# Input projection of a hybrid layer on one core: the weights of q, k, the convolution and the gates in column sets of 256 instead of 512

## The chip, the cores and the metric

The kernel runs on one NeuronCore of a Trainium2 chip. The metric is the device time of one execution in microseconds (us); it is compared by the median of several runs. PE is the matrix engine, PEld its weight loads, DVE the vector engine, ACT the scalar engine, POOL the GpSimd engine, SP the queue that issues nearly all DMAs.

## The reference, cut to what matters

One layer over 2048 tokens of width 1024. A normed input `u` goes through one wide projection; its columns are cut into q, k, v, a gate g, a low-rank gate, and the three parts of a gated short convolution. The rest (output projection, feed-forward, embedding gate) is not touched by the change.

```python
u = _rmsnorm(h, ln1_g[i])
proj = u @ w_in[i]
q, k, v, g, g_lr, cb, cc, cx = jnp.split(proj, offsets, axis=-1)
gate_logits = (g_lr @ w_gate_up[i] + b_gate[i]).astype(jnp.float32)
log_a = jax.nn.log_sigmoid(gate_logits) / GATE_NORMALIZER
...
o = _gla_chunked(qh, kh, vh, ah).astype(x.dtype)      # chunked linear attention (GLA)
o = _rmsnorm(o, gn_g[i]) * jax.nn.silu(gh)
y = cb * _causal_depthwise_conv(cc * cx, conv_w[i])
mix = jnp.concatenate([o, y], axis=-1) @ w_out[i]
```

## The kernel before, in words

All matrix products run in a split form: each float32 operand is cut into a high and a low part, and three products (high*high, high*low, low*high) are summed in PSUM. To cut a weight tile, ACT casts the raw float32 tile to the high part (L105) and DVE subtracts it from the raw one for the low part (L106). The pair of parts stands in a tile of the pool `hl`, the raw weights in a tile of the pool `raw`.

The first of three phases (`mixing_phase`) takes the tokens in four blocks of 512, numbered 0 to 3 here. In each block `mixing` does, in this order: the values v with the low-rank gate (weights as the moving operand), then 20 *units* of the transposed projection: four for q and k, eight for the convolution (`cc` and `cx` in turn), four for g and four for cb. A unit is 24 matmuls of 128x512 (8 chunks of the 1024 input features, k-chunks, by 3 passes) into one PSUM bank, followed by a small evacuation. Then `block` does the output projection with `w_out`, which also loads the next block's input, norms it and turns it.

`tick` is called in the middle and at the end of each unit. It advances the generator `gla`, which puts the attention's own small matmuls between the units: the gate logits (L370, in the middle of the second q/k unit), the score products of six levels (L417 for the first two, L427 for the others) and of pairs (L454), and then the state passes. Ahead of them stands a chain on ACT, POOL and DVE: absolute value, Exp and Ln of the logits (L371 to L375), differences on POOL (L377), a scan on DVE (L378), and per level two differences on POOL (L399, L400), an Exp on ACT (L401) and two products on DVE (L402, L403).

Weights come in *sets* by `weights`: a set of 512 columns is loaded by `load_pair`, two k-chunks to a raw tile (512 KB, rows of 2 KB; for the convolution two DMAs of 256 KB with rows of 1 KB), and `split` cuts one k-chunk of 512 columns at a time, so that a set is eight `hl` tiles, each of which serves all four units of the set.

```python
pools(st, {"hl": 11, "raw": 4, "w4": 13})
```

The pool `hl` has 11 tiles and `raw` has 4; a new tile takes the place of the one 11 (4) before it and waits until that one's last reader is done. In this phase only PE's instructions stand in the order in which the program is written. The order on ACT, DVE, POOL and SP is made by a scheduler ahead of the run, by a cost model of its own; on the chip each engine then runs its list strictly in order.

Of the kernel before, what the change touches and what calls it, by code (L numbers as in the profile page):

```python
# [8 lines left out]
F32 = mybir.dt.float32  # L9
F32R = mybir.dt.float32r  # L10
# [4 lines left out]
P = 128  # L15
S = 2048
D = 1024
NK = D // P
# [6 lines left out]
O_Q, O_V, O_G, O_LR, O_CB, O_CC, O_CX = 0, 512, 1024, 1536, 1552, 2064, 2576  # L25
# [14 lines left out]
def hybrid_layer(ctx: ExitStack, tc: tile.TileContext,  # L40
                 x, p, ln1_g, w_in, w_gate_up, b_gate, conv_w, gn_g, w_out, ln2_g,
                 w_up, w_down, ln3_g, w_pg, w_pp, lnf_g, out):
    nc = tc.nc
    x, out = x[0], out[0]
    p = p[0, 0]
    w_in, w_gate_up, b_gate, conv_w = w_in[0], w_gate_up[0], b_gate[0], conv_w[0]
# [5 lines left out]
    pl = {}  # L52
# [40 lines left out]
    def load_pair(src, k0, width, segs):  # L93

        raw = pl["raw"].tile([P, 2, width], F32, name="raw")
        o = 0
        for c, n in segs:
            nc.sync.dma_start(out=raw[:, :, o:o + n],
                              in_=src[k0 * P:(k0 + 2) * P, c:c + n].rearrange("(k p) n -> p k n", p=P))
            o += n  # L100
        return raw

    def split(raw, width):
        hl = pl["hl"].tile([P, 2, width], F32R, name="hl")
        nc.scalar.copy(out=hl[:, 0, :], in_=raw)  # L105
        nc.vector.tensor_tensor(out=hl[:, 1, :], in0=raw, in1=hl[:, 0, :].bitcast(F32), op=ALU.subtract)  # L106
        return hl

    def weights(src, segs, k0=0, nk=NK, between=None):
        width = sum(n for _, n in segs)  # L110
        tiles = []
        for k in range(k0, k0 + nk, 2):
            raw = load_pair(src, k, width, segs)
            if between:
                between(k)
            for i in range(2):
                tiles.append(split(raw[:, i, :], width))
        return lambda k, s: tiles[k][:, s, :]

# [31 lines left out]
    def unit(out_ap, lhs, rhs, nk, done=None, ticks=True):  # L153

        product(out_ap, lhs, rhs, nk, mid=True)
        if done is not None:
            done()
        if ticks:
            tick()

    def split_into(hi, lo, src):
        nc.scalar.copy(out=hi, in_=src)  # L162
        nc.vector.tensor_tensor(out=lo, in0=src, in1=hi.bitcast(F32), op=ALU.subtract)  # L163
# [4 lines left out]
    def uT_at(u, sl):  # L168
        return lambda k, s: u[k // 4][:, k % 4, s, sl]

    def tok_of(ti):
        return slice(ti * P, (ti + 1) * P)

    full = slice(0, T)
# [121 lines left out]
    def mixing_phase(st):  # L296
# [251 lines left out]
        def mixing(b, u1, first):  # L548

            vt = [w4([P, 2, 512]) for _ in range(2)]  # L550
            wv = weights(w_in, [(O_V, 512), (O_LR, 16)], between=first)

            def v_done(ps, ti, n):
                dst = vt[ti // 2][:, ti % 2, :]
                if n == 0:
                    nc.scalar.copy(out=dst[:, 0:264], in_=ps[:, 0:264])
                    return
                lr = tiny.tile([P, 16], F32, name="lr")
                nc.vector.tensor_copy(out=lr, in_=ps[:, 248:264])
                nc.scalar.copy(out=dst[:, 264:512], in_=ps[:, 0:248])  # L560

                def low_rank():
                    tp = tr_bank()
                    nc.tensor.transpose(out=tp[0:16, 0:P], in_=lr, identity=ident)
                    nc.vector.tensor_copy(out=lrT[0:16, ti * P:(ti + 1) * P], in_=tp[0:16, 0:P])
                later(2, low_rank)

            for ti in range(NT):
                if first is not None:
                    first(8 + ti)  # L570
                cols = [slice(n * 264, (n + 1) * 264) for n in range(2)]
                banks = [mm_bank() for _ in range(2)]
                lhs = uT_at(u1, tok_of(ti))
                if first is not None and ti == 0:
                    for k in range(NK):
                        for n in range(2):
                            for i, (a, c) in enumerate(PASSES):
                                nc.tensor.matmul(out=banks[n][:, 0:264], lhsT=lhs(k, a), rhs=wv(k, c)[:, cols[n]],
                                                 start=(k == 0 and i == 0), stop=(k == NK - 1 and i == 2))
                    v_done(banks[0], ti, 0)  # L580
                    v_done(banks[1], ti, 1)
                    continue
                for n in range(2):
                    unit(banks[n][:, 0:264], lhs, lambda k, s: wv(k, s)[:, cols[n]], NK,
                         lambda: v_done(banks[n], ti, n))
            mix = [None, None]
            wq = weights(w_in, [(O_Q, 512)])
            qT = w4([P, 2, T])
            kT = w4([P, 2, T])
            gsT = [w4([P, 2, T]) for _ in range(2)]  # L590
            side[0] = gla(qT, kT, vt, gsT, mix)
            for j in range(4):
                ps = mm_bank()

                def qk_done():
                    if j < 2:
                        nc.scalar.mul(out=qT[:, j, :], in_=ps, mul=0.125)
                    else:
                        nc.scalar.copy(out=kT[:, j - 2, :], in_=ps)
                unit(ps, lambda k, s: wq(k, s)[:, j * P:(j + 1) * P], uT_at(u1, full), NK, qk_done)  # L600

            mix[1] = big([P, 4, 2, T], F32R)
            yt = [w4([P, 2, T]) for _ in range(2)]
            for g in range(2):
                wc = weights(w_in, [(O_CC + g * 256, 256), (O_CX + g * 256, 256)])
                for jj in range(2):
                    j = g * 2 + jj
                    z = t2([P, T + 2])
                    pc = mm_bank()

                    def cc_done():
                        nc.gpsimd.tensor_copy(out=z[:, 0:2], in_=halo[:, j, :])
                        nc.scalar.copy(out=z[:, 2:T + 2], in_=pc)
                    unit(pc, lambda k, s: wc(k, s)[:, jj * P:(jj + 1) * P], uT_at(u1, full), NK, cc_done)
                    px = mm_bank()

                    def cx_done():
                        nc.vector.tensor_tensor(out=z[:, 2:T + 2], in0=px, in1=z[:, 2:T + 2], op=ALU.mult)
                        nc.gpsimd.tensor_copy(out=halo[:, j, :], in_=z[:, T:T + 2])
                        y = yt[g][:, jj, :]  # L620
                        nc.vector.tensor_scalar(out=y, in0=z[:, 2:T + 2], scalar1=cw[:, 2, j:j + 1], scalar2=None,
                                                op0=ALU.mult)
                        nc.vector.scalar_tensor_tensor(out=y, in0=z[:, 1:T + 1], scalar=cw[:, 1, j:j + 1], in1=y,
                                                       op0=ALU.mult, op1=ALU.add)
                        nc.vector.scalar_tensor_tensor(out=y, in0=z[:, 0:T], scalar=cw[:, 0, j:j + 1], in1=y,
                                                       op0=ALU.mult, op1=ALU.add)
                    unit(px, lambda k, s: wc(k, s)[:, 256 + jj * P:256 + (jj + 1) * P], uT_at(u1, full), NK, cx_done)
            wg = weights(w_in, [(O_G, 512)])
            for h in range(4):
                ps = mm_bank()  # L630

                def g_done():
                    gs = t2([P, T])
                    nc.scalar.activation(out=gs, in_=ps, func=AF.Silu)
                    nc.vector.tensor_scalar(out=gsT[h // 2][:, h % 2, :], in0=gs, scalar1=gng, scalar2=None, op0=ALU.mult)
                unit(ps, lambda k, s: wg(k, s)[:, h * P:(h + 1) * P], uT_at(u1, full), NK, g_done)

            wb = weights(w_in, [(O_CB, 512)])
            for j in range(4):
                ps = mm_bank()  # L640

                def cb_done():
                    y = yt[j // 2][:, j % 2, :]
                    last["cb"] = nc.vector.tensor_tensor(out=y, in0=ps, in1=y, op=ALU.mult)
                    split_into(mix[1][:, j, 0, :], mix[1][:, j, 1, :], y)
                unit(ps, lambda k, s: wb(k, s)[:, j * P:(j + 1) * P], uT_at(u1, full), NK, cb_done)
            while side[0] is not None:
                tick()
            return mix
# [30 lines left out]
        u1 = new_uT()  # L680
# [48 lines left out]
        for b in range(NB):  # L729
            u1 = block(b, u1, start if b == 0 else None)  # L730
# [691 lines left out]
```

## Time and profile before

| what | value |
|---|---|
| median of 3 runs | 2488.64 us (2488.27 to 2496.26) |
| the profiled execution: time, span | 2492.06 us, 2490.3 us |
| PE busy, share of the span | 2380.4 us, 96% |
| mean granted TensorE clock | 0.983 |
| DVE, ACT, POOL busy | 56%, 39%, 28% |
| raw weight loads from `w_in` of 512 KB / 256 KB | 64 / 64 |

The profile is one execution on the chip. In its groups a row has line, engine, operation, out<-in with the shapes, the count, the busy time, the mean time of one, and the idle time of the engine ahead of it with what ended it. The first phase ends at about 957 us.

### The profile page before, as it was taken

What the parts mean: (1) busy time and instruction counts of PE and PEld (TensorE: products, weight loads), DVE (VectorE), ACT (ScalarE), POOL (GpSimd) and SP (SyncE); (2) the same over time, 40 slices, a digit from 0 to 9 for tenths busy, and PEclk for the clock granted to TensorE, in tenths of its full rate; (3) what the DMA queues carried; (4) which work ended last, traced back from release to release, by engine and by line L of the source; (5) the groups of instructions that cost most, each with busy time, mean ns of one, the idle gap of its engine ahead of it and who ended that gap; (6) DMA issues with size and microseconds to landing.
All of it is one profiled execution on the core that took longest, in us unless ns stands there. A gap on an engine that the chain in (4) does not pass through costs nothing.

```text
span 2490.3 us, 31389 instructions
## 1 busy us (share of the span) xinstructions
PE 2380.4 (96%) x11752; PEld 1946.6 (78%) x11752; DVE 1394.1 (56%) x1676; ACT 974.7 (39%) x1533; POOL 698.6 (28%) x604
## 2 busy tenths in 40 slices
PE   7999999899999996999999999999999999999976
PEld 6777878777887784788888888888887888788765
DVE  4656465556646641655555664445546555655758
ACT  4434433443344333522222332222224344435555
POOL 3301210431103014244343243244522105301421
PEclk9999999999999997999999999999999999999988
DMA  4226323731542248854354576557757669756997
GB/s 154 68 68 217 103 72 135 217 99 59 170 153 68 68 145 274 277 175 164 135 181 162 196 260 217 202 200 256 259 203 288 201 220 296 276 189 239 330 298 273
DMA packets 274761, 471.08 MB, mean 189 GB/s; under 512 B 22688, under 2 KB 146096, under 8 KB 274608
## 3 DMA queue, kind: packets, MB, share of 16 engines
q1 hardware_dynamic: 272112, 460.66, 54.8%
q0 software_dynamic: 2496, 8.41, 1.4%
q8 instruction: 92, 1.51, 0.2%
q14 instruction: 61, 0.50, 0.1%
HBM read 326.92 MB, written 142.08 MB: 188 GB/s over the span
## 4 chain that ended last, share of the span: by engine, by line
PE 64%; DMA 7%; issue 3%; DVE 3%; ACT 2%; POOL 2%; SPq 0%; POOLq 0%; ACTq 0%; DVEq 0%
PE mm L148 46%; PE ps L1069 15%; DMA ur<-up 1%; DMA mr<-hid 1%; DMA mr<-u 1%; PE g L427 1%; DMA out_dram<-w 1%; POOL as L218 1%; DMA h<-h_out 1%; DMA w<-up 1%; POOL w L218 0%; DMA emb<-w 0%; DVE hl L106 0%; ACT mh L162 0%; PE ps L1102 0%
## 5 line engine op out<-in xcount | busy, mean ns | idle before, releaser
L1069 PE MATMUL ps<-wh,mh 128*128 128x512 f32 x2496 | 578.1, 392 | 23.2 <-ACT mh L162 16.0
L1069 PEld LDWEIGHTS ps<-wh,mh 128*128 128x128 f32 x2496 | 468.7, 189 | 126.3 <-ACT mh L162 18.0
L148 PE MATMUL mm<-uT,hl 128*128 128x512 f32 x1920 | 481.7, 405 | 10.1 <-DVE hl L106 6.3
L148 PE MATMUL mm<-uT,wu 128*128 128x512 f32 x2112 | 482.3, 389 | 0.0
L148 PEld LDWEIGHTS mm<-uT,wu 128*128 128x128 f32 x2112 | 396.5, 188 | 82.2
L148 PEld LDWEIGHTS mm<-uT,hl 128*128 128x128 f32 x1920 | 356.5, 190 | 105.1 <-DVE hl L106 11.8
L148 PE MATMUL mm<-U,wu 128*128 128x512 f32 x1584 | 364.5, 390 | 3.1 <-DVE v L218 3.1
L148 PEld LDWEIGHTS mm<-U,wu 128*128 128x128 f32 x1584 | 298.5, 188 | 65.6 <-issue 3.5
L163 DVE TENSOR_TENSOR wu<-raw,wu 128x1024 fp32r<-128x1024 f32 x154 | 218.1, 1416 | 209.3 <-ACT wu L162 208.8
L148 PE MATMUL mm<-hl,uT 128*128 128x512 f32 (+1 forms) x1584 | 301.0, 349 | 3.4 <-DVE uT L163 2.1
L148 PEld LDWEIGHTS mm<-hl,uT 128*128 128x128 f32 x1584 | 252.1, 190 | 42.8 <-DVE uT L163 2.7
L162 ACT CAST wu<-raw 128x1024 fp32r<-128x1024 f32 x154 | 161.5, 1050 | 304.7 <-PE mm L148 222.1
L163 DVE TENSOR_TENSOR wh<-wr,wh 128x1024 fp32r<-128x1024 f32 x111 | 141.3, 1273 | 235.8 <-ACT wh L162 235.0
L218 DVE TENSOR_TENSOR v<-mm,v 128x512 f32<-128x512 f32 x220 | 150.9, 687 | 151.4 <-PE mm L148 150.6
L218 POOL TENSOR_TENSOR v<-v,v 128x512 f32<-128x512 f32 x88 | 137.5, 1563 | 302.4 <-DMA hid<-v 262.0
L162 ACT CAST wh<-wr 128x1024 fp32r<-128x1024 f32 x111 | 110.8, 998 | 248.3 <-PE ps L1069 185.5
L106 DVE TENSOR_TENSOR hl<-raw,hl 128x512 fp32r<-128x512 f32 (+1 forms) x260 | 183.6, 744 | 26.5 <-ACT hl L105 26.3
L105 ACT CAST hl<-raw 128x512 fp32r<-128x512 f32 (+1 forms) x260 | 153.8, 622 | 61.3 <-PE mm L148 30.3
L218 POOL TENSOR_TENSOR raw<-raw 128x1024 f32<-128x1024 f32 x44 | 107.4, 2451 | 224.7 <-issue 149.3
L163 DVE TENSOR_TENSOR mh<-mr,mh 128x1024 fp32r<-128x1024 f32 x111 | 144.2, 1299 | 5.7 <-ACT mh L162 5.2
L162 ACT CAST mh<-mr 128x1024 fp32r<-128x1024 f32 x111 | 110.6, 996 | 9.4 <-DMA mr<-hid 7.2
L218 POOL TENSOR_TENSOR ur<-ur 128x512 f32<-128x512 f32 x60 | 93.5, 1559 | 31.7 <-DMA ur<-in_w_ple_gate_dram 26.9
(190 smaller groups left out, 1882.6 us busy)
## 6 DMA issues: line engine op xcount, KB each, us to landing
raw<-in_w_gate_upffn_dram SPq DMA_DIRECT2D x77, 512.0 KB, 4.8
hid<-v SPq DMA_DIRECT2D x154, 256.0 KB, 3.4
mr<-hid SPq DMA_DIRECT2D x70, 512.0 KB, 4.8
raw<-in_w_in_dram SPq DMA_DIRECT2D x64, 512.0 KB, 4.4
wu<-raw SPq DMA_DIRECT2D x44, 512.0 KB, 3.0
raw<-wu SPq DMA_DIRECT2D x44, 512.0 KB, 5.8
wr<-wd SPq DMA_DIRECT2D x40, 512.0 KB, 3.7
w<-in_x_dram SPq DMA_DIRECT2D x32, 512.0 KB, 9.0
```

The source lines that it names most:

```text
L105: nc.scalar.copy(out=hl[:, 0, :], in_=raw)
L106: nc.vector.tensor_tensor(out=hl[:, 1, :], in0=raw, in1=hl[:, 0, :].bitcast(F32), op=ALU.subtract)
L148: nc.tensor.matmul(out=out_ap, lhsT=lhs(k, a), rhs=rhs(k, b), start=(start and k == 0 and i == 0), stop=(k == nk - 1 and i == 2), **kw)
L162: nc.scalar.copy(out=hi, in_=src)
L163: nc.vector.tensor_tensor(out=lo, in0=src, in1=hi.bitcast(F32), op=ALU.subtract)
L218: return e.tensor_tensor(out=out, in0=a, in1=b, op=op)
L427: nc.tensor.matmul(out=sp[par][:, a, :], lhsT=X[r, c], rhs=X[r, c], start=True, stop=True)
L1069: nc.tensor.matmul(out=bk[n][t], lhsT=M[a][:, j, tok_of(t)], rhs=W[c][:, j, :], start=(on is None and k == 0 and i == 0), stop=(k == nk - ...
```

## The change

A new helper `columns` takes the place of `weights` for all of the input projection but the values. A set is 256 columns: two raw tiles, each with four k-chunks, and four `hl` tiles, each with two k-chunks. A set serves two units and is asked for just ahead of them. For the convolution the set of one j holds 128 columns of `cc` and 128 of `cx`. The number of raw tiles, of casts and subtractions, their sizes (128x512) and the bytes are as before. The output projection and the values keep `weights`.

```diff
+    def columns(src, segs, nk=NK):
+
+        tiles = []
+        for k in range(0, nk, 4):
+            raw = pl["raw"].tile([P, 4, 256], F32, name="raw")
+            o = 0
+            for c, n in segs:
+                nc.sync.dma_start(out=raw[:, :, o:o + n],
+                                  in_=src[k * P:(k + 4) * P, c:c + n].rearrange("(k p) n -> p k n", p=P))
+                o += n
+            for i in range(0, 4, 2):
+                hl = pl["hl"].tile([P, 2, 2, 256], F32R, name="hl")
+                split_into(hl[:, 0], hl[:, 1], raw[:, i:i + 2, :])
+                tiles.append(hl)
+        return lambda k, s: tiles[k // 2][:, s, k % 2, :]
...
-            wq = weights(w_in, [(O_Q, 512)])
...
             for j in range(4):
                 ps = mm_bank()
+                if j % 2 == 0:
+                    wq = columns(w_in, [(O_Q + j * P, 256)])
...
-                unit(ps, lambda k, s: wq(k, s)[:, j * P:(j + 1) * P], uT_at(u1, full), NK, qk_done)
+                unit(ps, lambda k, s: wq(k, s)[:, tok_of(j % 2)], uT_at(u1, full), NK, qk_done)
...
             for g in range(2):
-                wc = weights(w_in, [(O_CC + g * 256, 256), (O_CX + g * 256, 256)])
                 for jj in range(2):
                     j = g * 2 + jj
+                    wc = columns(w_in, [(O_CC + j * P, P), (O_CX + j * P, P)])
...
-                    unit(pc, lambda k, s: wc(k, s)[:, jj * P:(jj + 1) * P], uT_at(u1, full), NK, cc_done)
+                    unit(pc, lambda k, s: wc(k, s)[:, 0:P], uT_at(u1, full), NK, cc_done)
...
-                    unit(px, lambda k, s: wc(k, s)[:, 256 + jj * P:256 + (jj + 1) * P], uT_at(u1, full), NK, cx_done)
+                    unit(px, lambda k, s: wc(k, s)[:, P:2 * P], uT_at(u1, full), NK, cx_done)
...
-            wg = weights(w_in, [(O_G, 512)])
...
+                if h % 2 == 0:
+                    wg = columns(w_in, [(O_G + h * P, 256)])
...
-            wb = weights(w_in, [(O_CB, 512)])
...
+                if j % 2 == 0:
+                    wb = columns(w_in, [(O_CB + j * P, 256)])
```

The lists of the engines show what the scheduler made of it. PE's list is the same, instruction for instruction. Three places differ that matter below. In these lists the numbers tell one tile from another; a raw or `hl` tile is given when it is loaded or cut.

The first is ACT at the passage from q/k to the convolution, here in block 1. Before, the casts of the convolution's first set (raw_2739, raw_2748, raw_2757; the two of its first raw tile stand further up) from its fourth tile on stand behind two of the Exps of the levels (L401):

```order
L371 ACTIVATE uT_2619<-g_2650,bg_233 128x512
L374 ACT_TABLE_LOAD
L374 ACTIVATE uT_2619<-uT_2619 128x1024
L597 ACTIVATE w4_2598<-mm_2633 128x512
L375 ACT_TABLE_LOAD
L375 ACTIVATE uT_2619<-uT_2619 128x1024
L387 ACT_TABLE_LOAD
L387 ACTIVATE ebl_2673<-w4_2618 128x8
L401 ACTIVATE uT_2619<-uT_2619 128x1024
L599 COPY w4_2599<-mm_2675 128x512
L401 ACTIVATE uT_2619<-uT_2619 128x1024
L105 CAST hl_2745<-raw_2739 128x512
```

With the change the lines of the file are 16 higher (L387 is the old L371, L391 the old L375, L403 the old L387) and the list at the same place is:

```order
L614 ACTIVATE w4_2566<-mm_2570 128x512
L178 CAST hl_2745<-raw_2739 128x512
L178 CAST hl_2809<-raw_2806 128x512
L387 ACTIVATE uT_2603<-g_2630,bg_233 128x512
L387 ACTIVATE uT_2603<-g_2634,bg_233 128x512
L390 ACT_TABLE_LOAD
L390 ACTIVATE uT_2603<-uT_2603 128x1024
L614 ACTIVATE w4_2566<-mm_2617 128x512
L391 ACT_TABLE_LOAD
L391 ACTIVATE uT_2603<-uT_2603 128x1024
L178 CAST hl_2812<-raw_2806 128x512
L178 CAST hl_2818<-raw_2815 128x512
```

Here hl_2745 is the fourth and last tile of the convolution's first set (j = 0), and hl_2809, hl_2812 and hl_2818 are three of the four of its second (j = 1): they have moved ahead of the Exps of the levels, and two of them ahead of the logits' first operation.

The second is SP at the end of a block, here block 1: after the loads of `w_out` come those of the residual rows and gains, then the first weights of the next block's values (raw_4222).

```order
L98 DMA raw_3952<-in_w_out_dram 128x2x512
L188 DMA w4_3724<-in_ln2_g_dram 128x1024
L256 DMA w4_3726<-in_x_dram 128x1024
L256 DMA w4_3728<-in_x_dram 128x1024
L256 DMA w4_3730<-in_x_dram 128x1024
L256 DMA w4_3732<-in_x_dram 128x1024
L188 DMA w4_3734<-in_ln1_g_dram 128x1024
L256 DMA w4_3796<-in_x_dram 128x1024
L98 DMA raw_4222<-in_w_in_dram 128x2x512
```

With the change:

```order
L98 DMA raw_3952<-in_w_out_dram 128x2x512
L98 DMA raw_4222<-in_w_in_dram 128x2x512
L204 DMA w4_3724<-in_ln2_g_dram 128x1024
L272 DMA w4_3726<-in_x_dram 128x1024
L272 DMA w4_3728<-in_x_dram 128x1024
L272 DMA w4_3730<-in_x_dram 128x1024
L272 DMA w4_3732<-in_x_dram 128x1024
L204 DMA w4_3734<-in_ln1_g_dram 128x1024
L272 DMA w4_3796<-in_x_dram 128x1024
```

The load of 512 KB for the values has moved ahead of the seven loads of rows and gains.

The third is DVE in the convolution, block 1, between two score products of one level (the copies by mask32 empty the two PSUM banks of the attention, and the next score products wait for both). Before:

```order
L429 COPY_PREDICATED s_sb01_241<-mask32_244,g_3058 128x512
L618 TENSOR_TENSOR t2_2959<-mm_3036,t2_2959 128x512
L621 TENSOR_SCALAR w4_2729<-t2_2959,cw_234 128x512
L623 SCALAR_TENSOR_TENSOR w4_2729<-t2_2959,cw_234,w4_2729 128x512
L429 COPY_PREDICATED s_sb10_242<-mask32_244,g_3086 128x512
L625 SCALAR_TENSOR_TENSOR w4_2729<-t2_2959,cw_234,w4_2729 128x512
L429 COPY_PREDICATED s_sb11_243<-mask32_244,g_3087 128x512
```

With the change:

```order
L445 COPY_PREDICATED s_sb01_241<-mask32_244,g_3040 128x512
L179 TENSOR_TENSOR hl_3345<-raw_3340,hl_3345 128x512
L635 TENSOR_TENSOR t2_2941<-mm_3018,t2_2941 128x512
L179 TENSOR_TENSOR hl_3350<-raw_3348,hl_3350 128x512
L638 TENSOR_SCALAR w4_2729<-t2_2941,cw_234 128x512
L445 COPY_PREDICATED s_sb10_242<-mask32_244,g_3068 128x512
L640 SCALAR_TENSOR_TENSOR w4_2729<-t2_2941,cw_234,w4_2729 128x512
L445 COPY_PREDICATED s_sb11_243<-mask32_244,g_3069 128x512
```

Two subtractions of weight tiles (hl_3345, hl_3350) now stand among them, and one step of the convolution (L642, the old L625) has moved behind the last copy.

More of the change, by code (lines that the diff above doesn't have):

```diff
@@ L635, in g_done @@
                     nc.vector.tensor_scalar(out=gsT[h // 2][:, h % 2, :], in0=gs, scalar1=gng, scalar2=None, op0=ALU.mult)
-                unit(ps, lambda k, s: wg(k, s)[:, h * P:(h + 1) * P], uT_at(u1, full), NK, g_done)
-            wb = weights(w_in, [(O_CB, 512)])
+                unit(ps, lambda k, s: wg(k, s)[:, tok_of(h % 2)], uT_at(u1, full), NK, g_done)
             for j in range(4):
                 ps = mm_bank()
+                if j % 2 == 0:
+                    wb = columns(w_in, [(O_CB + j * P, 256)])
                 def cb_done():
@@ L645, in cb_done @@
                     split_into(mix[1][:, j, 0, :], mix[1][:, j, 1, :], y)
-                unit(ps, lambda k, s: wb(k, s)[:, j * P:(j + 1) * P], uT_at(u1, full), NK, cb_done)
+                unit(ps, lambda k, s: wb(k, s)[:, tok_of(j % 2)], uT_at(u1, full), NK, cb_done)
             while side[0] is not None:
```

## The prediction

> **What bounds the kernel now.** I read the page's first part, its groups, the idle time ahead of PE's groups, then PE's timeline of the first phase and a table of stretches.
>
> ```profile
> PE 2380.4 (96%) x11752; PEld 1946.6 (78%) x11752; DVE 1394.1 (56%) x1676; ACT 974.7 (39%) x1533; POOL 698.6 (28%) x604
> L148 PE MATMUL mm<-uT,hl 128*128 128x512 f32 x1920 | 481.7, 405 | 10.1 <-DVE hl L106 6.3
> ```
>
> PE is busy for 96% of the span, and no other engine is near it, so time can only be won where PE stands still or runs slowly. The second row is the group that the change feeds: all 80 units, 1920 matmuls. PE idled 10.1 us ahead of them, mostly until DVE had finished a weight tile. The timeline of block 2 shows where:
>
> ```profile
> 516.72 16.66 PE L148 MATMUL mm<-uT,hl 128*128 128x512 f32 x69
> 533.89 0.72 PE L148 MATMUL mm<-uT,hl 128*128 128x512 f32 x2 [0.51 <-ACT hl L105]
> 535.80 0.97 PE L148 MATMUL mm<-uT,hl 128*128 128x512 f32 x3 [1.19 <-DVE hl L106]
> 537.25 0.96 PE L148 MATMUL mm<-uT,hl 128*128 128x512 f32 x3 [0.48 <-DVE hl L106]
> 538.81 18.64 PE L148 MATMUL mm<-uT,hl 128*128 128x512 f32 x67 [0.60 <-DVE hl L106]
> 557.39 0.68 PE L417 MATMUL g<-uT 64*64 64x64 f32 x16
> ```
>
> The stretch starts behind the gate logits, in the middle of the second q/k unit. 12 matmuls end that unit, 48 more are the last two of q/k, so the 69th is the ninth of the first convolution unit: PE has used three k-chunks, and waits for the fourth tile of the convolution's set. ACT's timeline says why it is late:
>
> ```profile
> 516.46 0.69 ACT L371 ACTIVATE uT<-g,bg 128x512 f32<-128x512 f32 x1 [3.05 <-PE g L370]
> 530.23 1.06 ACT L401 ACTIVATE uT<-uT 128x1024 f32<-128x1024 f32 x1 [1.93 <-POOL uT L400]
> 531.20 0.57 ACT L599 COPY w<-mm 128x512 f32<-128x512 f32 x1
> 532.27 1.06 ACT L401 ACTIVATE uT<-uT 128x1024 f32<-128x1024 f32 x1 [0.51 <-POOL uT L400]
> 533.24 2.68 ACT L105 CAST hl<-raw 128x512 fp32r<-128x512 f32 x5
> ```
>
> The five casts run at 533.24, behind two Exps that wait for POOL. They could not have been put much earlier: with 11 tiles, the fourth tile of this set takes the place of the first of q/k, which is read until the last q/k unit. The stretch from the logits to the first score product, 144 matmuls, compares the blocks (rows 1 to 4), with a run of 96 undisturbed matmuls (row 5) and three short windows inside the stretches of blocks 1, 2 and 3 (length, PE busy, ..., granted clock):
>
> ```profile
> core 0: us, PE busy (x) PEld busy (x) DVE busy (x) ACT busy (x) POOL busy (x), PEclk, DMA share, GB/s
> 55.43:93.26 37.83, 35.10 (x146) 26.78 (x145) 23.34 (x27) 19.87 (x28) 17.34 (x14) 1.00 0.19 56
> 281.90:320.70 38.80, 36.63 (x146) 27.66 (x145) 25.06 (x27) 21.08 (x29) 18.22 (x14) 0.96 0.19 54
> 516.72:557.39 40.67, 37.89 (x147) 28.76 (x145) 25.06 (x27) 21.09 (x29) 18.24 (x14) 0.92 0.18 52
> 745.77:784.74 38.97, 36.52 (x147) 27.50 (x145) 25.06 (x27) 21.09 (x29) 18.23 (x14) 0.96 0.18 54
> 656.30:678.70 22.40, 22.40 (x97) 17.99 (x96) 8.22 (x12) 7.14 (x14) 2.04 (x4) 1.00 0.81 284
> 302.50:306.00 3.50, 3.49 (x8) 2.30 (x9) 3.50 (x5) 2.63 (x5) 0.87 (x1) 0.51 0.65 197
> 538.10:544.90 6.80, 6.20 (x15) 4.79 (x15) 6.80 (x12) 2.45 (x4) 0.11 (x1) 0.50 0.67 191
> 766.80:770.20 3.40, 3.11 (x8) 1.89 (x8) 3.40 (x6) 2.20 (x4) 0.45 (x1) 0.50 0.64 197
> ```
>
> The stall costs more than its idle time: right behind it, in three of four blocks, the clock granted to PE is halved for 3.4 or 6.8 us.
>
> **The change part by part.** *The fourth tile.* An undisturbed matmul takes 22.40 / 96 = 0.2333 us, 144 of them 33.60. The four stretches lose 37.83 - 33.60 = 4.23, 5.20, 7.07 and 5.37 us, 21.87 in all. A part is not the stall's: the first 69 matmuls take 16.66 us where (68 x 0.2333) + 0.39 for the last one's own duration would be 16.26; this 0.40 at the start stays, 1.6 in four blocks. That leaves 20.3 us to win: idle time (37.83 - 35.10) + 2.17 + 2.78 + 2.45 = 10.1; half speed over 3.5, 6.8 and 3.4 us, about 1.7 + 3.4 + 1.7 = 6.8; the remaining 3.4 is the refilling of PE's pipeline after each stop.
>
> Will it be won? In the change the convolution's first set has four tiles. The first three take the places of value tiles. The fourth takes that of q/k's first tile, which now is read for the last time early in the second unit, not in the fourth; its cast (hl_2745) stands ahead of the logits' first operation, where ACT idled 3.05 us (516.46), some 17 us ahead of PE's need at 533.4. Of the second set, needed two units (11.2 us) later still, three casts stand ahead of the Exps too, the last behind two of them. Had that one come as late as the five at 533.24, it would still be in time: PE would reach the set at 516.72 + 0.40 + 108 x 0.2333 = 542.3, and its last tile 18 matmuls later, at 546.5. All later sets are asked for with about two units to spare: the last tile of a set takes the place of the first tile of the set three before. So I take the whole 20.3. If only the idle time and the refills went, it would be 13.5; the ends are 0 and 20.3, and the value is near the upper one by the row of casts.
>
> *The chain of the attention.* PE comes to the first score product earlier by up to 6.7 us (block 2: 550.7 instead of 557.39). Its inputs are ready by:
>
> ```profile
> 544.70 0.68 DVE L403 TENSOR_TENSOR uT<-uT,w 128x512 f32<-128x512 f32 x1
> ```
>
> That is 545.4, 5.3 us ahead. The two casts ahead of the logits (2 x 0.62) run in ACT's idle time; so 0.
>
> *The copies of the scores (third place above).* Two subtractions come between two copies, one step of the convolution moves behind. Before, the same pattern one level on makes PE wait a little:
>
> ```profile
> 595.82 0.71 DVE L429 COPY_PREDICATED s_sb<-mask,g 128x512 f32<-128x512 uint8 x1
> 596.17 1.57 PE L427 MATMUL g<-uT 64*128 64x128 f32 x16
> L106 DVE TENSOR_TENSOR hl<-raw,hl 128x512 fp32r<-128x512 f32 (+1 forms) x260 | 183.6, 744 | 26.5 <-ACT hl L105 26.3
> ```
>
> The score products at 596.17 take 1.57 us since their bank is emptied only at 596.5. In the change that place has fewer subtractions, the earlier one has two more (0.74 each by the group's mean), with one step of the convolution less. At most 0.4 is won at the one and 0.7 lost at the other per block, -1.6 to +2.8 us in four; taken as 0.
>
> *Loads.* The raw tiles of `w_in` come in rows of 1 KB instead of 2 KB, for the convolution of 512 B instead of 1 KB.
>
> ```profile
> raw<-in_w_in_dram SPq DMA_DIRECT2D x64, 512.0 KB, 4.4
> raw<-in_w_in_dram SPq DMA_DIRECT2D x64, 256.0 KB, 4.0
> up<-w SPq DMA_DIRECT2D x56, 256.0 KB, 2.6
> 478.17 1.11 SPq L98 DMA_DIRECT2D raw<-in_w_in_dram  x2
> 484.24 1.97 PE L203 MATMUL tr<-ident,w 128*128 128x128 f32 x8 [3.51 <-ACT w L234]
> ```
>
> 256 KB in rows of 1 KB land in 4.0 us, as many bytes in pieces of 512 B (stores) in 2.6: small pieces don't set the time here, and DMA is busy for 19% of these stretches. At one place PE waits for such a load: between blocks 1 and 2 ACT must first cast a q/k tile whose load is issued at 478.17, before it empties a bank for the transposes at 484.24. That load now has 512 pieces of 1 KB; no row shows it. Between 4.0 us (256 such pieces, so -0.4) and twice that (+3.6) I take +0.5, nearest to the 512 KB row.
>
> *The values' load ahead of the rows (second place).* At a block's end DMA is saturated:
>
> ```profile
> 657.00:673.00 16.00, 16.00 (x70) 12.91 (x69) 3.54 (x6) 1.74 (x3) 0.00 (x0) 1.00 0.99 355
> 672.09 1.06 ACT L179 ACTIVATE w<-w 128x1024 f32<-128x1024 f32 x1 [14.08 <-DMA w<-in_x_dram]
> 674.25 1.28 DVE L196 SCALAR_TENSOR_TENSOR w<-w,rs,w 128x1024 f32<-128x1024 f32 x1 [5.85 <-POOL rs L183]
> 678.70 1.03 PE L203 MATMUL tr<-ident,w 128*128 128x128 f32 x8
> ```
>
> 512 KB (524,288 bytes) at 355 GB/s are 1.5 us, by which the next block's rows land later than at 672.09. Their norm ends at 675.5, PE wants it at 678.70: 3.2 us of room, so 0. Queued behind the moved load are seven loads; it waits for the cut of a raw tile of `w_out`, which DVE's list has ahead of the last cb product that releases those loads anyway.
>
> *Sum:* -20.3 + 0 + 0 + 0.5 + 0 = -19.8; 2492.06 - 19.8 = 2472.3 for the profiled execution. It is 3.4 us above the median of the runs. If those have the same stalls, 2488.64 - 19.8 = 2468.8; if one half-speed window of 6.8 us is what they lack (3.4 us), 16.4 is won, 2472.2. I take 2470.
>
> **The rivals.** *The half clock stays.* Its windows might follow from something other than the stall; then only idle time and refills go, 13.5 - 0.5 = 13.0: 2475.6. For it: block 0 has a stall as long (2.7) at full clock. Against: the three windows start at 302.5, 538.1 and 766.8, inside the stalls, each time. The Trainium skill (TensorE: Matmul & The Clock Gate, section HAM oscillation) asks for PE idle gaps above about 3.4 us before the clock drops, and the stops here are at most 1.2 us: by that rule the windows are not the stall's and the time is this rival's. The same page (Part 1) describes a free-running window of 3413 ns that sets the clock by activity; the lengths of 3.4 and 6.8 us agree with that.
>
> *The stall moves on by one set.* The last tile of the second set, behind two Exps, is late in its turn; if half is lost again, 10 us are won: 2478.6. Against it are the 13 us between 533.24 and 546.5.
>
> *No gain.* Two casts now stand ahead of the logits on ACT. If the second set's load lands late, they hold up the attention's whole chain; from 5.3 us of delay on PE waits at the first score product, and at 10 us late the gain is eaten: 2488. Against: such loads land in 4.0 us.
>
> *Slower.* At the ends of blocks 0 to 2 the moved load holds the seven behind it back until its raw tile is free. From 3.2 - 1.5 = 1.7 us on PE waits for the transposes; for a net loss it takes (19.8 + 7.5) / 3 = 9 us more at each end, some with half clock behind it. With 11 us late: about 2497 to 2502. Against: the release is a cut that ended beside the last cb product.
>
> **How the numbers follow.** Whole stall gone 0.70 (2463 to 2475, by the -1.6 and +2.8 of the copies, the +3.6 of the load and the 3.4 between runs); half clock stays 0.11; moves on 0.07; no gain 0.07; slower 0.05. The range of 2462 to 2479 holds the first three. A measurement of this kernel tells about 0.3% (7.5 us) from no change; the first three cases are faster by more: 0.88, same 0.07, slower 0.05.
>
> **What would show it.** Right: the stretch of 144 matmuls takes about 34 us in every block, PE's idle ahead of `mm<-uT,hl` falls from 10.1 to under 1 us, the clock reads 1.00 in all four stretches, and the casts and subtractions of `hl` keep their counts of 260. Wrong: an idle ahead of a later convolution unit, ahead of L417, or ahead of L203 with ACT behind a load.

## The result, and the profile after

The changed kernel takes 2473.06 us (median of 4 runs, 2472.65 to 2473.37); the kernel before takes 2489.24 us in the same comparison (4 runs, 2488.27 to 2496.26). The ratio is 0.9929, 95% interval 0.9911 to 0.9947: 16.2 us faster. The forecast was 2470.0 us, with a range of 2462 to 2479. The profiled executions stand closer to the working: their spans go from 2490.3 to 2470.9 us, 19.4 us less, where the sum said 19.8; the profiled time is 2472.65 us, forecast 2472.3.

First PE's row of the page after and the group that the change feeds (the old L148 is now L164):

```profile
PE 2371.9 (96%) x11752; PEld 1945.6 (79%) x11752; DVE 1400.7 (57%) x1676; ACT 974.8 (39%) x1533; POOL 712.9 (29%) x604
L164 PE MATMUL mm<-uT,hl 128*128 128x512 f32 x1920 | 472.1, 401 | 0.0
```

The idle ahead of the 1920 matmuls is 0.0 (it was 10.1), and they are busy for 9.6 us less. The table of stretches after, from the logits to the first score product, blocks 0 to 3:

```profile
core 0: us, PE busy (x) PEld busy (x) DVE busy (x) ACT busy (x) POOL busy (x), PEclk, DMA share, GB/s
55.77:89.86 34.09, 34.09 (x147) 27.05 (x145) 23.50 (x29) 19.51 (x28) 15.88 (x13) 1.00 0.33 93
280.35:314.44 34.09, 34.09 (x146) 27.05 (x144) 24.53 (x28) 20.38 (x29) 16.43 (x13) 1.00 0.33 93
511.05:545.14 34.09, 34.09 (x146) 27.05 (x144) 24.53 (x28) 20.37 (x29) 16.43 (x13) 1.00 0.33 93
733.82:767.91 34.09, 34.09 (x147) 27.05 (x145) 24.52 (x28) 20.38 (x29) 16.43 (x13) 1.00 0.33 93
```

Each stretch takes 34.09 us, all of it busy and at full clock. Together they go from 156.27 to 136.36 us, 19.9 us less, where the whole span lost 19.4: everything else together came out at about nothing. ACT's timeline in block 2 shows the casts that used to stand behind the Exps (now L417):

```profile
508.87 0.62 ACT L178 CAST hl<-raw 128x512 fp32r<-128x512 f32 x1 [1.14 <-PE mm L164]
509.98 0.62 ACT L178 CAST hl<-raw 128x512 fp32r<-128x512 f32 x1 [0.49 <-PE mm L164]
510.80 0.69 ACT L387 ACTIVATE uT<-g,bg 128x512 f32<-128x512 f32 x1 [0.20 <-PE g L386]
...
517.48 1.12 ACT L178 CAST hl<-raw 128x512 fp32r<-128x512 f32 x2
...
525.38 1.06 ACT L417 ACTIVATE uT<-uT 128x1024 f32<-128x1024 f32 x1 [2.29 <-POOL uT L416]
```

The convolution's fourth tile is cut at 508.87, as soon as PE has done with the q/k tile in its place; PE's first convolution unit begins at about 525.4. The next cast waits for PE too, and the logits' first operation after it still waits for PE's logits (0.20), not for the cast.

Two places moved, and the sum had not foreseen how. At the end of block 0 the transposes wait a little longer than before (first fence: after; second: before):

```profile
226.25 0.66 PE L219 MATMUL tr<-ident,w 128*128 128x128 f32 x4 [1.19 <-DVE uT L179]
227.85 0.97 PE L219 MATMUL tr<-ident,w 128*128 128x128 f32 x4 [0.94 <-ACT w L250]
```

```profile
229.65 0.66 PE L203 MATMUL tr<-ident,w 128*128 128x128 f32 x4 [0.96 <-DVE uT L163]
231.03 0.66 PE L203 MATMUL tr<-ident,w 128*128 128x128 f32 x4 [0.73 <-ACT w L234]
```

That is 0.44 us; at the ends of blocks 1 and 2 the same two stops grew by 0.66 and 0.56 us. Behind those of blocks 0 and 1 stands a window of half clock, 3.41 us from 228.06 and from 453.33, which this profile of the kernel before did not have. Between blocks 1 and 2 the stop became shorter instead:

```profile
479.70 1.21 PE L219 MATMUL tr<-ident,w 128*128 128x128 f32 x8 [3.05 <-ACT w L250]
```

It was 3.51 us; the half clock behind it lasts 3.41 us instead of 6.83.

### The profile page after: what moved, and what is told of

It is laid out like the page before. It is cut to its first block, busy times and chain, and to the rows that moved or that the text cites. A ratio compares the mean times of both kernels' runs of the same rounds, so it can differ in the third digit from the quotient of the medians.

```text
span 2470.9 us, 31385 instructions
## 1 busy us (share of the span) xinstructions
PE 2371.9 (96%) x11752; PEld 1945.6 (79%) x11752; DVE 1400.7 (57%) x1676; ACT 974.8 (39%) x1533; POOL 712.9 (29%) x604
## 4 chain that ended last, share of the span: by engine, by line
PE 65%; DMA 6%; DVE 3%; issue 2%; ACT 2%; POOL 2%; SPq 1%; POOLq 0%; DVEq 0%; ACTq 0%
PE mm L164 47%; PE ps L1088 15%; DMA out_dram<-w 1%; DMA ur<-up 1%; PE g L443 1%; DMA pp<-emb 1%; DMA mr<-u 1%; DVE mh L179 1%; DMA mr<-hid 1%; DMA w<-up 1%; POOL as L234 0%; DVE h L234 0%; POOL w L234 0%; DMA emb<-w 0%; PE ps L1121 0%
## 5 line engine op out<-in xcount | busy, mean ns | idle before, releaser
L1088 PEld LDWEIGHTS ps<-wh,mh 128*128 128x128 f32 x2496 | 469.2, 189 | 126.9 <-ACT mh L178 19.2
L164 PE MATMUL mm<-uT,wu 128*128 128x512 f32 x2112 | 482.3, 389 | 0.0
L164 PE MATMUL mm<-uT,hl 128*128 128x512 f32 x1920 | 472.1, 401 | 0.0
L164 PEld LDWEIGHTS mm<-uT,wu 128*128 128x128 f32 x2112 | 396.6, 188 | 82.1
L164 PEld LDWEIGHTS mm<-uT,hl 128*128 128x128 f32 x1920 | 354.2, 188 | 87.3 <-issue 2.6
L164 PE MATMUL mm<-U,wu 128*128 128x512 f32 x1584 | 362.9, 389 | 2.2 <-DVE v L234 2.2
L164 PEld LDWEIGHTS mm<-U,wu 128*128 128x128 f32 x1584 | 297.4, 188 | 64.2 <-issue 2.6
L164 PE MATMUL mm<-hl,uT 128*128 128x512 f32 (+1 forms) x1584 | 303.7, 351 | 3.4 <-DVE uT L179 2.1
L164 PEld LDWEIGHTS mm<-hl,uT 128*128 128x128 f32 x1584 | 254.2, 191 | 43.4 <-DVE uT L179 2.7
L179 DVE TENSOR_TENSOR hl<-raw,hl 128x512 fp32r<-128x512 f32 x160 | 118.6, 765 | 49.6 <-ACT hl L178 49.4
L178 ACT CAST hl<-raw 128x512 fp32r<-128x512 f32 x160 | 93.8, 618 | 74.5 <-PE mm L164 62.6
```

Of the source, the lines that this page charges most:

```text
L164: nc.tensor.matmul(out=out_ap, lhsT=lhs(k, a), rhs=rhs(k, b), start=(start and k == 0 and i == 0), stop=(k == nk - 1 and i == 2), **kw)
L1088: nc.tensor.matmul(out=bk[n][t], lhsT=M[a][:, j, tok_of(t)], rhs=W[c][:, j, :], start=(on is None and k == 0 and i == 0), stop=(k == nk - ...
```

## The experiments

**Which part of the change does it?** Theory A is the prediction's: the tile is late because its cast stands on ACT behind Exps that wait for POOL, and it stands there because its place comes free late. Theory B: the convolution's own finer sets do it. Three kernels each apply `columns` to one part alone. The first:

```diff
-            wq = weights(w_in, [(O_Q, 512)])
+                if j % 2 == 0:
+                    wq = columns(w_in, [(O_Q + j * P, 256)])
```

> Only q and k are taken in sets of 256 columns; convolution, g and cb stay in sets of 512. Theory A (the convolution's fourth tile is late, because it takes the place of a q/k tile that is read until the last q/k unit, and so has its cast behind two Exps on ACT): with q/k in short sets the place is free 8 us earlier, ACT's list has five of the eight convolution casts ahead of the logits and two more ahead of the Exps; the stretches of 144 matmuls take 33.6 to 34.2 us in all four blocks, the idle ahead of mm<-uT,hl falls from 10.1 to under 1 us, and the time from 2489 to 2470 to 2474. Theory B (it is the convolution's own finer sets that help: its first unit then needs four tiles, not eight, before the Exps are through): the first unit still needs eight tiles here, so the stretches stay at 37 to 40 us and the time at 2486 to 2490.

Measured: 2475.0 us (2472.01 to 2480.91) against 2490.49, ratio 0.9945 (0.9929 to 0.9961). The stretches of blocks 0 and 1 (2 and 3 are like 1), PE's stop in block 0, and ACT there:

```profile
56.37:94.52 38.15, 36.16 (x147) 28.00 (x145) 22.50 (x26) 18.76 (x26) 17.71 (x14) 0.96 0.18 55
284.72:319.06 34.34, 34.34 (x147) 26.93 (x145) 24.24 (x26) 20.04 (x27) 18.41 (x14) 1.00 0.21 62
```

```profile
77.73 16.86 PE L164 MATMUL mm<-uT,hl 128*128 128x512 f32 x63 [1.91 <-ACT hl L105]
```

```profile
76.12 1.06 ACT L417 ACTIVATE uT<-uT 128x1024 f32<-128x1024 f32 x1 [0.58 <-POOL uT L416]
77.08 1.65 ACT L105 CAST hl<-raw 128x512 fp32r<-128x512 f32 x3
```

Three stalls are gone, so B is wrong as the only reason. In block 0 the expectation missed: PE now stops 21 matmuls into the unit, at the eighth tile, whose cast stands behind four Exps. It is A's mechanism at another tile, since the unit still needs all eight.

The second part alone, the convolution:

```diff
-                wc = weights(w_in, [(O_CC + g * 256, 256), (O_CX + g * 256, 256)])
+                    wc = columns(w_in, [(O_CC + j * P, P), (O_CX + j * P, P)])
```

> Only the convolution is taken in sets of 256 columns; q, k, g and cb stay in sets of 512. The fourth tile of its first set still takes the place of q/k's first tile and its cast still stands behind two Exps on ACT. But it now holds k-chunks 6 and 7, which PE reaches 18 matmuls into the unit and not 9: 535.3 us in block 2 instead of 533.2. Theory A: the tile was ready at about 535.7 us there, so a stop of about 0.4 us in block 2 and less in the others is left, and no half clock behind it: stretches of 33.6 to 34.5 us, time 2470 to 2475. Theory B says the same, 2470 to 2474, and differs in the run before. A third reading (the half clock follows from any stop at this place, however short) gives stretches of about 35.5 us in the three later blocks and a time of 2475 to 2479.

Measured: 2475.63 us (2470.34 to 2480.95), ratio 0.9942 (0.9923 to 0.996).

```profile
55.73:90.92 35.19, 34.62 (x146) 26.87 (x144) 24.50 (x30) 20.80 (x30) 15.68 (x13) 1.00 0.30 90
279.37:313.59 34.22, 34.22 (x146) 26.95 (x144) 23.91 (x27) 20.13 (x29) 15.32 (x12) 1.00 0.32 91
```

The late cast stays where it was, but PE needs the tile nine matmuls later: a stop of 0.46 us is left in block 0 and none in the others, with no half clock in the stretches. The time lies just above the expected 2470 to 2475 and inside the third reading's range, but the stretches of 34.2 us in the three later blocks decide: the third reading is wrong. Either part alone wins most of the time, by another way each; block 0 is clean only with both.

The third part alone, g and cb:

```diff
-            wg = weights(w_in, [(O_G, 512)])
-            wb = weights(w_in, [(O_CB, 512)])
+                    wg = columns(w_in, [(O_G + h * P, 256)])
+                    wb = columns(w_in, [(O_CB + j * P, 256)])
```

> Only g and cb are taken in sets of 256 columns; q, k and the convolution stay in sets of 512. Theories A and B: the stall at the first convolution unit is untouched (37.8 to 40.7 us for the stretches, idle of 10 us ahead of mm<-uT,hl). What the change gave back at the ends of blocks 0 and 1 (about 1.5 us each: half clock for 3.4 us behind the transposes) has two readings: it comes with the order at a block's end, which these sets of cb and g make, then it is here too, and the time is 2490 to 2494; or it comes with the earlier arrival of the blocks, then the windows at 228 and 453 us are not here, and the time is 2487 to 2490.

Measured: 2492.22 us (2483.86 to 2498.74) against 2490.49, ratio 1.001 (0.9998 to 1.0022): no gain, as expected. The stops at the end of block 0 are 0.97 and 0.73 us, as before the change. No half clock stands at 228 or 453 us, but one window does at 241, behind the next tile's transposes. The time fits the first reading of the block ends and the missing windows fit the second, so this run alone does not decide between them.

**Is it the order on ACT?** All sets as before the change; one dependency turns ACT's order round.

```diff
-                nc.scalar.activation(out=X, in_=X, func=AF.Exp, scale=1.0 / 16.0)
+                e = nc.scalar.activation(out=X, in_=X, func=AF.Exp, scale=1.0 / 16.0)
+                if i < 4:
+                    after(e, last["conv"])   # the cast of the first set's eighth tile
```

> All sets as before the change (512 columns); only the Exps of the first four levels must wait for the cast of the eighth tile of the convolution's first set, so that on ACT the casts of tiles four to eight stand ahead of the Exps instead of behind two of them. Theory A: the places come free between 526.2 and 531.1 us in block 2, the casts run from about 528.3 us, the fourth tile is ready by 530 where PE needs it at 533.2: stretches of 33.6 to 34.5 us, time 2470 to 2475, by the order on ACT alone. The Exps come 1 to 3 us later, which the 5.3 us ahead of the first score product cover. If A is wrong and the tiles' places themselves (or their loads) are what is late, the stall stays, the Exps come later on top of it, and the time is 2487 to 2495.

Measured: 2474.44 us (2468.18 to 2475.27), ratio 0.9934 (0.9919 to 0.9949). Stretches of blocks 0 and 2, then ACT in block 2:

```profile
56.30:90.39 34.09, 34.09 (x147) 27.02 (x146) 27.24 (x27) 19.95 (x28) 18.78 (x14) 1.00 0.21 62
509.62:544.05 34.43, 34.35 (x147) 26.93 (x145) 26.62 (x26) 20.73 (x29) 17.45 (x13) 1.00 0.21 62
```

```profile
521.59 2.70 ACT L105 CAST hl<-raw 128x512 fp32r<-128x512 f32 x5
524.38 1.06 ACT L401 ACTIVATE uT<-uT 128x1024 f32<-128x1024 f32 x1
```

With 512 columns, 11 places and the same loads, the five casts ahead of the Exps take the stall away. So the order on ACT is what cost the time. That the places only led the scheduler to that order is argued from the run with q and k alone, where they came free earlier and the list changed. The Exps run 14.76 us after the stretch's start instead of 13.51, and no stop of PE follows from it.

**What is the half clock?** In the prediction it was a price of three stalls. Two kernels were profiled once more, the changed one and the one before.

> The changed kernel once more, on the chip of the next three runs, to compare with. If the half clock behind a short stop depends on how the stop falls into a running grid of 3.41 us windows (theory G: a window in which PE is busy for less than about 52% halves the clock of the next one, and the grid's phase differs between executions), the lengths of the stretches and the idle times repeat to 0.1 us, but the halved windows of the short stops need not stand where they stood (228, 453, 480, 2102 us); by the busy shares of its trace about 45% to 50% of the phases halve a window at each block end, 34% at the next tile's transposes. If instead each stop has its fixed penalty (theory F), they stand where they stood. Time 2470 to 2476.

Measured: 2471.43 us (2470.44 to 2473.44), ratio 0.9921 (0.9906 to 0.9937). The stretches repeat at 34.09 us.

```profile
228.00:231.40 3.40, 3.40 (x16) 2.77 (x15) 1.12 (x2) 0.54 (x1) 0.00 (x0) 1.00 0.51 154
237.00:240.40 3.40, 3.40 (x11) 2.79 (x10) 2.22 (x3) 1.34 (x3) 0.00 (x0) 0.50 0.53 151
452.00:455.40 3.40, 3.40 (x11) 2.81 (x12) 1.78 (x2) 0.59 (x1) 1.35 (x2) 0.50 0.69 203
```

The window at 228 us is at full clock now, and one stands at 237 behind the next tile's transposes; that at 452 has stayed, as has the one between blocks 1 and 2 (now at 479), and that at 2102 is gone.

> The kernel before, profiled a second time. Theory G (windows of 3.41 us on a running grid; a window in which PE is busy for less than about 52% halves the next): the four stalls repeat to about 0.3 us in their idle time, and the half clock behind them comes in some blocks and not in others, not necessarily in blocks 1, 2 and 3; by the busy shares of the first trace 81% of the phases do it in block 0 and 66% in the others. Theory F (the half clock is a fixed price of these three stalls): blocks 1, 2 and 3 again, not block 0.

Measured: one run, 2493.37 us. Three pairs of consecutive windows, at the stalls of blocks 0, 2 and 3:

```profile
72.49:75.90 3.41, 1.21 (x6) 0.53 (x4) 1.51 (x2) 2.54 (x4) 2.88 (x3) 1.00 0.00 0
75.90:79.30 3.40, 3.01 (x7) 1.98 (x7) 3.40 (x7) 3.40 (x7) 0.00 (x0) 0.51 0.46 143
...
536.75:540.16 3.41, 1.74 (x7) 0.88 (x6) 3.41 (x3) 3.41 (x7) 3.41 (x3) 1.00 0.22 53
540.16:543.57 3.41, 3.15 (x8) 1.98 (x7) 3.41 (x6) 2.27 (x4) 0.53 (x1) 0.50 0.62 192
761.99:765.40 3.41, 1.95 (x8) 0.94 (x6) 2.83 (x3) 3.32 (x6) 3.41 (x4) 1.00 0.00 0
765.40:768.80 3.40, 2.11 (x7) 1.15 (x8) 3.40 (x4) 2.80 (x5) 2.62 (x2) 1.00 0.53 154
```

The stall of block 0 is followed by half clock this time and that of block 3 isn't; in block 2 it lasts 3.41 us, not 6.8. The first stops repeat (2.20 us in block 0; 0.5 and then about 1.2 us in the others); the shorter ones behind them vary. What decides is how much of one window PE was busy in: 1.21 and 1.74 us of 3.41 (35% and 51%) halve the next, 1.95 us (57%) does not. Within each trace all halved windows start on one grid of 3.413 us. Over the twelve traces of this study (15 to 2440 us of each) 76 of the 85 full-clock windows with PE busy below 51.5% are followed by half clock, and 2 of the 8238 above it. (Busy time is that of PE's matmul records; the nine that are not followed lie between 43% and 51.5% busy.) So G holds, not without exceptions, and F is wrong. One exception is block 0 of the first profile of before, 47% busy and yet no half clock behind it:

```profile
70.47:73.88 3.41, 1.62 (x7) 0.96 (x6) 1.32 (x2) 1.69 (x3) 3.41 (x4) 1.00 0.00 0
```

**What lengthens the block ends?** The changed kernel without its third part:

```diff
-                    wg = columns(w_in, [(O_G + h * P, 256)])
-                    wb = columns(w_in, [(O_CB + j * P, 256)])
+            wg = weights(w_in, [(O_G, 512)])
+            wb = weights(w_in, [(O_CB, 512)])
```

> q, k and the convolution in sets of 256 columns, g and cb in sets of 512: the changed kernel without its third part. Theory A: the stretches of 144 matmuls stay at 34.1 us. On DVE the block ends have the order they had before the change (a row's residual ahead of the next norm); in the changed kernel and with g and cb alone the norm comes first. If that order is what lengthens the stops at the block ends by 0.45 us, they are 0.96 + 0.73 us here as before and the share of grid phases that halve a window falls to about a third at one place per block end; time 2468 to 2474, 0 to 4 us below the changed kernel. If the values' load alone lengthened them, they stay at 1.2 + 0.94 us.

Measured: 2473.08 us (2467.5 to 2475.7), ratio 0.9926 (0.991 to 0.9942).

```profile
226.27 0.66 PE L219 MATMUL tr<-ident,w 128*128 128x128 f32 x4 [0.96 <-DVE uT L179]
227.66 0.66 PE L219 MATMUL tr<-ident,w 128*128 128x128 f32 x4 [0.73 <-ACT w L250]
```

The stops are as before the change, though the block ends as early as in the changed kernel. With g and cb alone the order is the changed one and the stops are short too. So it takes the third part together with a block that arrives earlier: by about 3.5 us at the end of block 0 and 6.5 to 7 at that of block 1. In the lists the third part changes two things there, the order on DVE (a norm ahead of the residual) and the place of the values' load. ACT at the end of block 0 tells them apart (first the changed kernel, then this one):

```profile
217.43 1.06 ACT L195 ACTIVATE w<-w 128x1024 f32<-128x1024 f32 x1 [3.58 <-DMA w<-in_x_dram]
221.57 1.06 ACT L195 ACTIVATE w<-w 128x1024 f32<-128x1024 f32 x1 [2.04 <-DVE w L687]
```

```profile
217.45 1.06 ACT L195 ACTIVATE w<-w 128x1024 f32<-128x1024 f32 x1 [3.36 <-DMA w<-in_x_dram]
218.98 1.06 ACT L195 ACTIVATE w<-w 128x1024 f32<-128x1024 f32 x1
```

The row for the first norm lands at the same time in both, so the moved load did not hold it back. The next norm's square then waits 2.04 us for DVE's residual in the changed kernel and for nothing here, so at this place it is the order. In the time the 0.44 us can't be seen: the intervals of the two kernels overlap.

The half clock at the end of block 0 does not need the longer stops. Here the stops are short, and yet a window of half clock follows them; the second profile of the kernel before has one at the same place (first this kernel, then that one):

```profile
228.48:231.90 3.42, 3.42 (x10) 2.65 (x9) 0.94 (x2) 0.45 (x1) 0.00 (x0) 0.50 0.51 153
232.95:236.37 3.42, 3.42 (x11) 2.84 (x12) 1.63 (x2) 0.58 (x1) 0.00 (x0) 0.50 0.44 133
```

At the end of block 1 only the two profiles of the changed kernel have one, where the stops are longest; that fits theory G, but two profiles do not show it.

**What holds the load between blocks 1 and 2?** The stores of the computed operands of the norm (four a tile) go out by POOL's queue. First on the sets of 512 with the later Exps, then on the kernel just above:

```diff
-            put = lambda n, t: nc.sync.dma_start(out=ops[n][:, :, tok], in_=t)
+            put = lambda n, t, e=nc.sync: e.dma_start(out=ops[n][:, :, tok], in_=t)
-            put(5, s[:, 0])
+            put(5, s[:, 0], g)             # g = nc.gpsimd; 6, 7 and 4 likewise
```

> Sets as before the change (512 columns), the Exps of four levels behind the convolution's casts (as in the run with that alone), and the stores of the four computed operands (5, 6, 7 and 4) in the norm for the up projection issued by POOL, which computes them, not by SP. Question: what holds the q/k load between blocks 1 and 2, ahead of which PE stops for 3.0 to 3.5 us, always with half clock behind it? Theory Q: it is SP's queue, which waits in these stores for POOL (9 us in one row) with the load of q/k behind them; then the load is issued as soon as its raw tile is free, the stop at 478 us falls to under 1 us, and 3 to 6 us are won: 2466 to 2471. Rival R: it is the raw tile, free only when the values' tiles are cut; then the stop stays, and the time is 2470 to 2476, or more if POOL's issuing delays its own arithmetic.

> q, k and the convolution in sets of 256 columns, g and cb in sets of 512, and the four stores issued by POOL. If A, the reading of the block ends and Q hold together, nothing is left of the convolution stall, of the longer block ends, or of the stop between blocks 1 and 2: 2463 to 2470, the fastest so far, 3 to 9 us below the changed kernel. If R holds, 2468 to 2474.

Measured: 2470.36 us (2469.12 to 2472.74), ratio 0.9918 (0.9903 to 0.9934), and 2467.53 us (2467.05 to 2471.22), ratio 0.9908 (0.989 to 0.9926). SP's queue in the changed kernel, then the same place in the second of the two, on SP and on PE:

```profile
464.86 8.30 SPq L251 DMA_DIRECT2D up<-w  x5
473.24 1.18 SPq L127 DMA_DIRECT2D raw<-in_w_in_dram  x2
```

```profile
464.00 7.96 SPq L127 DMA_DIRECT2D raw<-in_w_in_dram  x3
```

```profile
470.38 4.65 PE L164 MATMUL mm<-hl,uT 128*128 128x264 f32 x32 [2.11 <-DVE hl L106]
477.08 1.06 PE L219 MATMUL tr<-ident,w 128*128 128x128 f32 x8 [2.05 <-DVE lr L575]
```

Q holds for the load: it is issued from 464.00 on, not at 473.24. But Q's other forecast, a stop of under 1 us, missed: the stop of 3.05 us turned into two of 2.1 us (2.10 and 0.90 in the first of the two kernels), for weight tiles and a copy on DVE, so little was won. DVE's five subtractions there took 8.80 us (1.21, 3.70, 2.81 and twice 0.69), 6.56 in the same kernel with the stores on SP; the mean of one before the change is 0.744:

```profile
462.76 8.80 DVE L106 TENSOR_TENSOR hl<-raw,hl 128x528 fp32r<-128x528 f32 x5
...
466.92 1.53 POOL L251 DMA_DIRECT2D up<-w  x2
468.24 1.51 POOL L234 TENSOR_TENSOR w<-w,w 128x512 f32<-128x512 f32 x1
```

The last kernel keeps that only for block 1 (`q = g if ops is up_ops[0] else nc.sync`), since at the end of block 3 PE had a new stop of 2.98 us.

> q, k and the convolution in sets of 256 columns, g and cb in sets of 512, and the four stores issued by POOL in block 1 only; in block 3 SP issues them as before. In the run with both blocks' stores on POOL, PE got a new stop of 3 us at the end of block 3 (a norm's transposes waited for an ACT copy), with half clock for 6.8 us behind it. If it is the issuing on POOL that made it, it is gone here: 2464 to 2467. If it comes from the order of the lists, it stays: 2467 to 2471.

Measured: 2473.38 us (2470.11 to 2476.28) against 2492.11, ratio 0.9926 (0.9912 to 0.9939). The stop at the end of block 3 is gone, so it came from the issuing on POOL, and the next phase's first products with `wu` start at 987.30 us, 2.25 earlier than with both on POOL. By 1029 us only 0.3 us of that is left, since a stop for DVE behind them takes 3.28 us instead of 1.30; the time missed the expectation. The lowest median of all is that of the kernel with both blocks' stores on POOL, 3.9 us below the changed kernel on one chip, but the two intervals overlap; that it is faster is not established.

## Why the prediction was right, and where it was off

**The fourth tile** (-20.3): right in place, cause and size. The stretches won 19.9, with 0.49 us a block staying instead of 0.40. The cause was only argued from the order; the run with the later Exps shows it, and the runs with one part alone show that two repairs lie in the change, an earlier place (q and k) and a later need (the convolution). The 3.4 us that the sum put down to refilling went with the stops, but no run isolates what they consist of. That the sum and the profiled difference agree to 0.4 us is partly luck: it rests on one draw of the half clock, as the next point tells, and on small terms that cancelled.

**The half clock in it** (6.8 of the 20.3): it belongs to the stall, as taken, but is no fixed price. Three profiles of the same stalls lost 21.9, 19.2 and 18.6 us (g and cb alone: 153.01 - 134.4), with 13.7, 10.2 and 6.8 us of halved windows in the stretches. The sum was worked from the dearest draw of the three. The Trainium skill (TensorE: Matmul & The Clock Gate, HAM oscillation) has idle gaps above about 3.4 us as the condition, the rival of 2475.6: the rows speak against it, since in blocks 1 to 3 stops of at most 1.2 us that add up to some 1.7 us within one window were enough. Its Part 1, the free-running window of 3413 ns, is what the grid shows. The prediction's "at most 1.2 us" does not hold for block 0, whose first stop is 2.20 us; that too is below 3.4, and half clock follows it in two of the three profiles.

**From the profiled execution to the median** (2472.3 or 2468.8, taken 2470): mis-sized. 16.2 us were won by the medians of the first comparison and 19.2 on another chip (2490.65 to 2471.43). The grid's draw is a candidate for the spread of the runs of before (2484.4 to 2497.0 in all later runs together), which no run isolates.

**The attention's chain** (0): right; PE comes to the first score product in block 2 at 545.14 and waits for nothing. **The copies of the scores** (0): about right. No idle stands ahead of either group of score products, as before, but this wait showed in their length, not in idle time: the group of L427 (now L443) is busy for 37.9 us instead of 38.9, and the products that took 1.57 us take 1.16, so 1.0 us was won, inside the range of -1.6 to +2.8.

**Loads** (+0.5): wrong in sign (3.51 to 3.05 us) and in reason. The smaller pieces cost nothing here: raw tiles of 512 KB land in 4.0 us instead of 4.4. What holds the load back is SP, which stands in stores that wait for POOL with the load behind them; that queue was not looked at. Why the stop became 0.46 us shorter was not isolated.

**The values' load ahead of the rows** (0): right for the load itself, since at the end of block 0 the row lands no later. But the stops there grew by 0.44 to 0.66 us at three block ends, where DVE's list changed at the same place (shown above for block 0) and the blocks arrive earlier; the step looked at the load's time alone. The half clock behind two of them, some 3 us in this profile, is a draw at block 0's end and may belong to the longer stops at block 1's.

## What to carry to other kernels

When a tile is late, look at what its cast stands behind in its engine's list before resizing buffers or sets: one dependency that lets the cast go first won about as much as the whole change. Behind short stops, don't charge a fixed half-clock price: add up the idle time within 3.41 us (here about 1.65 us was the limit), and profile twice before a difference of a few us is given a cause. A load that comes late may be held by the waits of whatever stands ahead of it on its queue, and moving those to another queue moves their cost too.

## What was not expected of the hardware

The halving rule above, with a sharp step near 51.5% of PE's busy time in one 3.413 us window, and a grid whose phase differs between executions. And the weight subtraction on DVE: of those between 462 and 473 us in the kernels with q, k and the convolution by columns, it takes 0.68 to 0.71 us alone, 1.73 to 1.80 beside POOL's products (stores on SP) and up to 3.7 where POOL issues its stores between them. The Trainium skill (SBUF — State Buffer, section SBUF: two separate sides) calls the port pair that the two engines share an exclusive lock, held for a whole instruction, also between a DVE operation with two SBUF inputs and a POOL operation that reads SBUF. The subtractions beside POOL's products agree with that: they take about as long as one product, 1.6 to 1.8 us.
